# Five more seven-product pairs in a hybrid encoder layer on one Trainium2 core, with earlier sums and an unspread gate

## The chip, the core and the metric

The kernel runs on one core of a Trainium2 chip (trn2). A core has a matrix engine (TensorE, PE in the profile, with its weight loads as PEld), a vector engine (VectorE, DVE), a scalar engine (ScalarE, ACT), GpSimd (POOL) and SyncE (SP), which issues the DMAs of the weights. Each engine works through its own queue in the order of the program, and they wait for each other by semaphores. The metric is the time of one execution in device microseconds; lower is better.

## The reference

One layer of an encoder over 256 tokens of width 4096, all in float32. `h` is the normalised input; one wide projection `h @ w_in` gives latents for q and kv (1024 and 512), a rotary key (64), and gates, q, k, v for two groups of 16 heads of width 128. Group A is latent attention, group B a banded (dilated) attention over q, k, v taken straight from the projection.

```python
h = rms_norm(x, g_mix)
c_q, c_kv, k_rope, gate_a, q_b, k_b, v_b, gate_b = split(h @ w_in)
y_a = mla_attention(q from c_q @ w_uq, k and v from c_kv @ w_ukv)
y_a = rms_norm(y_a, g_out_mla) * silu(gate_a)
y_b = dilated_mixture_attention(q_b, k_b, v_b)
y_b = rms_norm(y_b, g_out_dil) * silu(gate_b)
x = x + concat(y_a, y_b) @ w_out
gate = sigmoid(rms_norm(x, g_ple) @ w_ple_gate)
x = x + (p @ w_ple) * gate
out = rms_norm(x, g_final)
```

## The kernel before, in words

**Operands in two halves.** TensorE multiplies in the reduced type fp32r. To keep float32's accuracy, every operand is split in two: `hi`, the value rounded to fp32r by ACT (L115), and `lo`, the rest, by a subtraction on DVE (L116). A product of two tiles is then three matmuls (`mm`, L133 to L135: hi times hi, hi times lo, lo times hi, of 512 columns). For weights this costs ACT and DVE one pass each over every tile that the DMA brings (`raw`).

**Blocks of 1024 columns.** A `Block` computes 256 tokens by 1024 columns of output over 32 tiles of 128 weight rows, as four quarters of 128 by 512. There are two ways to take weight rows:

- A *plain step* (`plain_step`) takes one tile of rows: four products, so eight for two tiles, and one pass of ACT and DVE over 1024 columns.
- A *fast pair* (`fast_steps`) takes two tiles of rows in four steps and needs seven products instead of eight (the scheme of Strassen and Winograd). It needs sums and differences of the four pieces of the weights, which DVE makes (four subtractions of 512 columns, L833, into a temporary tile), and of the four pieces of the left operand, which a task makes beforehand (`add_sums`, L871, with a split on ACT and DVE). So a pair has four conversions: 512 columns in the first step, 1024 in each of the others. The second step's hi half is written at L846 and its lo half at L848.

`weave(fast, lead, trail)` writes out the order of a block: `lead` plain steps, then the fast pairs with the other plain steps spread among them (the plain step stands behind the first of a pair's four), then `trail` plain steps. At the end of a block there are the tasks `mid` (when the fast products are complete) and `done`.

**The order of the program** is one list, `steps`, run from top to bottom (the loop at the end). The parts, in time: the latents and the gates of group A; 64 steps of `w_uq` and `w_ukv` beside the first half of the gate columns, in which the 16 latent heads run; the last gate columns (`ga3`, 16 steps); six blocks for q, k, v of group B (two for each, `d_mid` and `d_done`); 64 steps of group B's gate beside its heads; three blocks of `w_out` and 32 steps for its last columns; four wide blocks of `w_ple_gate` with `w_ple` (`wide_mid`, `wide_done`, `wide_ple`; the fourth has quarters of 384 columns); and the last 256 columns. The blocks of this text: the *first q block* is the first of the six; *output blocks* one to three are those of `w_out`; *wide blocks* one to four those of `w_ple_gate`.

**Lead.** At step i the loop converts up to step i + 2, or i + 5 where the block's ring has more than three places; then it emits step i's products, then calls `advance`. The *ring* names the buffers for converted operands: three of a pool (`wp`) and, where there is room, tiles that other stages leave free (`B6`, `B4`, `Ah2`, `Al1`...). A step gets no buffer until the step that had it before has run. `phase` sets the place in the ring with which a block begins; without it the count goes on. Raw tiles come by DMA, four at a time at most.

**Tasks.** Everything beside the products is a generator. `advance` (one *tick* for each step) resumes every task once, so a task's `yield` puts the rest of it behind the next step. A head (`attend`, from L409) takes one tick each for its transpositions, splits, scores, softmax, normalisation, transpositions, splits, products with v, and copy; it is flagged at its end (`("head", dil, h)`). Two heads start two ticks apart. `x_sums` makes the eight sums of x for the six q, k, v blocks, two ticks each, in tiles that the latent heads use (`T0` to `T7`, with `B0` as temporary); it waits for the last latent head, and its eighth sum for `("gated", 3)`. `y_stats` (L557) computes the root mean square of an attention's output through `rsqrt_mean` (L225, which yields three times), and `gating` (from L571) then works through four groups of heads: a scaling on ACT (L578), transpositions on PE (L585), products on DVE (L593). `wide_done` (L1063) computes a wide block's gate from four quarters: a tanh on ACT (L1084), a product on DVE (L1086), an addition to the residual (L1088), a square on ACT (L1091). From its third round on it waits five ticks in a round, except in the last block.

Of the kernel before, what the change touches and what calls it, by code (L numbers as in the profile page):

```python
# [20 lines left out]
NT = S // P  # L21
DM = 4096
HEADS = 16
# [55 lines left out]
def encoder_layer(ctx: ExitStack, tc: tile.TileContext, x, p, positions, g_mix, w_in, g_q_latent, w_uq,  # L79
# [329 lines left out]
    def attend(h, q_src, k_src, pe, v, y, dil):  # L409

        tp = turn_bank([4, P])
        for t in range(NT):
            nc.tensor.transpose(tp[:, t], q_src(t), ident)
            nc.tensor.transpose(tp[:, NT + t], k_src(t), ident)
        yield
        qk = slot(f"T{h % 2}", [2, 4 * P], F32R)
        split(qk[:, 0], qk[:, 1], tp.rearrange("p a b -> p (a b)"))  # L420
        if dil:
            flags.add(("read", h))
        yield
        s = bank("s", [NT, S])
        for t in range(NT):
            a = tuple(qk[:, i, t * P:(t + 1) * P] for i in range(2))
            b = tuple(qk[:, i, S:] for i in range(2))
            mm(s[:, t], a, b, True, pe is None)
            if pe is not None:
                both = pe[0]()[:, t * P:(t + 1) * P]  # L430
                nc.tensor.matmul(s[:, t], both, pe[1][0], start=False, stop=False)
                nc.tensor.matmul(s[:, t], both, pe[1][1], start=False, stop=True)
        yield
        i = h % 2
        e = E["t"][:, i]
        nmax, l, rl = E["s"][:, i, 0], E["s"][:, i, 1], E["s"][:, i, 2]
        if not dil:
            nc.vector.tensor_reduce(nmax, s, axis=AX.X, op=ALU.max, negate=True)
            for t in range(NT):
                nc.scalar.activation(e[:, t], s[:, t], AF.Exp, bias=nmax[:, t:t + 1], accum_out=l[:, t:t + 1])  # L440
        else:
            flat = "p a b -> p (a b)"
            nc.vector.scalar_tensor_tensor(e.rearrange(flat), E["d"][:, 0].rearrange(flat), -SLOPES[h],
                                           s.rearrange(flat), op0=ALU.mult, op1=ALU.add)
            nc.vector.tensor_reduce(nmax, e, axis=AX.X, op=ALU.max, negate=True)
            yield
            for t in range(NT):
                nc.scalar.activation(e[:, t], e[:, t], AF.Exp, bias=nmax[:, t:t + 1])
            yield
            for t in range(NT):  # L450
                nc.vector.scalar_tensor_tensor(e[:, t], e[:, t], 1.0, E["d"][:, 1, t], op0=ALU.mult,
                                               op1=ALU.mult, accum_out=l[:, t:t + 1])
            nc.vector.reciprocal(rl, l)
        yield
        if not dil:
            nc.vector.reciprocal(rl, l)
        for t in range(NT):
            if dil:
                nc.scalar.activation(e[:, t], e[:, t], AF.Copy, scale=rl[:, t:t + 1])
            else:  # L460
                nc.vector.tensor_scalar(e[:, t], e[:, t], rl[:, t:t + 1], None, op0=ALU.mult)
        yield
        tp = turn_bank([NT, S])
        for k in range(NT):
            for t in range(NT):
                nc.tensor.transpose(tp[:, k, t * P:(t + 1) * P], e[:, t, k * P:(k + 1) * P], ident)
        yield
        pt = slot(f"T{2 + h % 2}", [2, NT, S], F32R)
        split(pt[:, 0], pt[:, 1], tp)
        if dil:  # L470
            vs = slot(("Q0", "T6")[h % 2], [2, NT, HD], F32R)
            split(vs[:, 0], vs[:, 1], v)
            v = lambda kt: (vs[:, 0, kt], vs[:, 1, kt])
        yield
        o = bank("o", [S])
        for k in range(NT):
            mm(o, v(k), tuple(pt[:, i, k] for i in range(2)), k == 0, k == NT - 1)
        yield
        nc.scalar.activation(y, by_token(o) if dil else o, AF.Copy)
        sq = junk[:, S * i:S * (i + 1)] if h else acc  # L480
        nc.scalar.activation(sq, o, AF.Square)
        if h:
            nc.gpsimd.tensor_tensor(acc, acc, sq, op=ALU.add)
        flags.add(("head", dil, h))
# [72 lines left out]
    def y_stats(dil):  # L557
        while not all(("head", dil, h) in flags for h in range(HEADS)):
            yield
        yield  # L560
        tp = turn_bank([2 * S])
        for t in range(NT):
            nc.tensor.matmul(tp[:, t:t + 1], acc[:, t * P:(t + 1) * P], ones, start=True, stop=True)
        yield
        yield from rsqrt_mean(ry[dil], tp[:, :NT], WIDTH)
        nc.vector.tensor_tensor(ry[dil], ry[dil], rxh, op=ALU.mult)
        flags.add(("ry", dil))

# [494 lines left out]
    def wide_done(k, blk):  # L1063
# [10 lines left out]
        def task():  # L1074
# [7 lines left out]
            for n in range(6):  # L1082
                for i, t, h, m in quarters[n:n + 1]:
                    nc.scalar.activation(e[:, i], e[:, i], AF.Tanh, scale=r1h[:, t:t + 1])  # L1084
                for i, t, h, m in quarters[n - 1:n] if n else ():
                    nc.vector.scalar_tensor_tensor(e[:, i], e[:, i], 1.0, P4[t, h][:, :blk.q], op0=ALU.add, op1=ALU.mult)  # L1086
                    for u, xc, at, _ in pieces(h, i):
                        nc.vector.tensor_tensor(xc[:, t, at], u, xc[:, t, at], op=ALU.add)  # L1088
                for i, t, h, m in quarters[n - 2:n - 1] if n > 1 else ():
                    for u, xc, at, c in pieces(h, i):  # L1090
                        nc.scalar.activation(u, xc[:, t, at], AF.Square, accum_out=ss2[:, t, c:c + 1])  # L1091
                for _ in range(5 if n > 1 and k < WIDE - 1 else 1):
                    yield
            if k == WIDE - 1:
                for t in range(NT):
# [162 lines left out]
    lay(blk, order, gates_mid(blk), gates_done(blk))  # L1258
    hook(len(steps), only("t0", "t1"))
    M = M[::-1]  # L1260
    ga2 = from_x(OFF_GA + 1024, 512, done_gate(0, 2))
    other, ga2.banks = M
    for i in range(8):
# [2 lines left out]
        add(ga2, 2 * i + 1, 2 * i + 2)  # L1266
        add(Chunk(cols(w_ukv, 512 * i, 512), 4, 512, lhs_c("kv"), other, done_uk(i), lambda j: ["latents"]))
    hook(len(steps), lambda: spawn(y_stats(0)))
    hook(len(steps) + 1, lambda: spawn(x_sums()))
    ga3 = from_x(OFF_GA + 1536, 512, done_gate(0, 3))  # L1270
    ga3.banks = M[1]
    add(ga3)
# [2 lines left out]
    z_tags = "T0", "T1", "T2", "T3", "T4", "T7", "T5", "T6"  # L1275

    def x_sums():
        while ("head", False, HEADS - 1) not in flags:
            yield
        z = lambda j: slot(z_tags[j], [2, 4, P], F32R)  # L1280
        yield from add_sums(7, x_pair, z, "B0", "x_sums", x_s)
        while ("gated", 3) not in flags:
            yield
        yield from add_sums(8, x_pair, z, "B0", "x_sums", x_s, first=7)

    tags = LAST
    for n, key in enumerate((key, i) for i in range(2) for key in "qkv"):
        off = {"q": OFF_Q, "k": OFF_K, "v": OFF_V}[key[0]] + 1024 * key[1]
        order = weave((range(5), range(8), range(8), range(8), (4, 5, 0, 1, 2, 3, 6, 7), (0, 1, 2, 3, 6, 7))[n],
                      16 if n == 0 else 2, 2)  # L1290
        ring = (["B6", "B4"], ["B4", "B6", "B0"], ["B4", "B6", "B0"], ["B4", "B6"], ["B4", ("T4", "T7")], [("T4", "T7")])[n]
        after = ((), (), ["B4", "B6"], ["B4"], [("T4", "T7")], ())[n]
        blk = Block(w_in[:, off:off + 1024], lhs_x, x_s, "x_sums", order, lambda kt: (), tags, "B1", WP + ring)
        lay(blk, order, d_mid(key, blk), d_done(key, blk), after=after, used={2: ("used", 5)} if n == 4 else {})
        if n == 0:
            steps[-len(order[1])].phase = 0
        tags = follow(tags)
    beside = [len(steps), len(steps) + 64]
    for c in range(4):
# [7 lines left out]
    for k in range(WIDE_O):  # L1307
        hook(len(steps), only(*(("t0", "t1"), ("m2", "m3"), ("m0", "m1"))[k]))
        for h in range(2):
            hook(len(steps) + 4 + h, lambda c=2 * k + h: load_res(c))  # L1310
        order = weave(*((range(4), 12, 4), (range(7), 6, 4), (range(6), 8, 4))[k])
        blk = Block(w_out[:, 1024 * k:1024 * (k + 1)], lhs_y, y_s, "y_sums", order, lambda kt: need_y(kt // 2),
                    tags, "Al2" if k < 2 else "Al1", WP + (["Ah2", "Al1"] if k < 2 else [("B7b", "T7")]))
        lay(blk, order, out_mid(k, blk), out_done(k, blk))
        tags = follow(tags)
    for c in (6, 7):
        hook(len(steps), lambda c=c: (load_res(c), only("t0", "t1")()))
# [4 lines left out]
    for k in range(WIDE):  # L1322
# [4 lines left out]
        if k == 3:  # L1327
            hook(len(steps), lambda: spawn(load_g()))
        lay(blk, order, wide_mid(k, blk), wide_done(k, blk), wide_ple(k, q), **({"after": [], "used": {4: "z used"}} if k == 3 else {}))
    small = Chunk(cols(w_ple, 3840, 256), 2, 256, lambda kt: (pT[0][:, 0, kt], pT[0][:, 1, kt]), ("t0", "t1"), done_p(8),  # L1330
                  lambda j: ["pT"])
    steps.insert(len(steps) - 2, (small, 0))
# [235 lines left out]
```

## Time and profile before

| | us |
|---|---|
| median of 3 runs | 1924.57 (1923.02 to 1925.47) |
| the profiled execution | 1922.93 |
| its span, first to last instruction | 1921.2 |

The profile is of one execution. An engine's busy time is the sum of its instructions, and a matmul's end is modelled, so busy times of matmuls overlap and the count over a stretch tells more than the busy share. In a timeline row stand the start and the duration in us, the engine, the line of the kernel, the operation, what it writes and reads (by the program's names, numbers left out), the shape, and how many such instructions follow each other; in square brackets idle time of the engine ahead of it and what ended it. In a row of a stretch stand the stretch, its length, then busy time and count of PE, PEld, DVE, ACT and POOL, the granted clock of PE, the DMA's share and its GB/s.

### The profile page before, as it was taken

Reading aid. Unit: us, or ns where it says so; the run is one execution under the profiler, and the core shown is the slowest. Engines: PE = TensorE matmul, PEld = TensorE weight load, DVE = VectorE, ACT = ScalarE, POOL = GpSimd, SP = SyncE. Lnnn points to the kernel's source line nnn. Section 1 sums busy time; section 2 is a strip of 40 time slices with the busy share of each in tenths; the row PEclk is TensorE's granted clock in tenths of the full one; section 3 lists DMA queues with packets and bytes.
Section 4 is the critical chain, followed back from the end, with each engine's and each line's share of the span. In section 5 each row is a group of like instructions: output and inputs, shape, how many; then the busy total and the mean of one; then the engine's idle time right before and its main releaser. Section 6 shows DMA issues by size and latency. Waiting matters only on the chain.

```text
span 1921.2 us, 25661 instructions
## 1 busy us (share of the span) xinstructions
PE 1905.4 (99%) x9246; PEld 1629.2 (85%) x9246; DVE 1589.1 (83%) x2221; ACT 1114.5 (58%) x1547; POOL 71.3 (4%) x115
## 2 busy tenths in 40 slices
PE   9999999999999999999999999999999999999997
PEld 8998889998888888888888888888888888888897
DVE  7877966665999999899877778889896698989897
ACT  6655555565555565655556666555565455566554
POOL 0001011220000000000000010000000000000000
PEclk9999999999999999999999999999999999999999
DMA  7666654445656666666664456665666556566565
GB/s 260 196 181 198 206 164 145 143 153 157 196 186 206 212 209 197 214 200 196 213 195 143 132 165 219 204 213 172 233 195 217 188 190 218 183 212 202 190 220 195
DMA packets 139350, 370.58 MB, mean 193 GB/s; under 512 B 12476, under 2 KB 33816, under 8 KB 139224
## 3 DMA queue, kind: packets, MB, share of 16 engines
q1 hardware_dynamic: 137816, 363.96, 59.5%
q0 software_dynamic: 1408, 5.00, 0.7%
q8 instruction: 72, 1.18, 0.2%
q14 instruction: 54, 0.44, 0.1%
HBM read 364.72 MB, written 4.19 MB: 192 GB/s over the span
## 4 chain that ended last, share of the span: by engine, by line
PE 93%; DVE 5%; ACT 1%; issue 1%; DMA 1%; DVEq 0%; ACTq 0%
PE m L134 19%; PE m L135 19%; PE m L133 19%; PE t L133 4%; PE t L134 4%; PE t L135 4%; PE s L134 3%; PE s L135 3%; PE s L133 3%; PE o L134 3%; PE o L135 3%; PE o L133 3%; DVE lo L116 1%; DVE B L833 1%; ACT hi L115 1%
## 5 line engine op out<-in xcount | busy, mean ns | idle before, releaser
L116 DVE TENSOR_TENSOR lo<-raw,hi 128x1024 fp32r<-128x1024 f32 (+5 forms) x478 | 519.3, 1092 | 191.4 <-ACT hi L115 188.5
L115 ACT ACTIVATE hi<-raw 128x1024 fp32r<-128x1024 f32 (+5 forms) x478 | 454.0, 954 | 336.7 <-PE m L135 152.1
L133 PE MATMUL m<-hi,Ah 128*128 128x512 f32 (+3 forms) x1001 | 383.5, 383 | 0.0
L134 PE MATMUL m<-lo,Ah 128*128 128x512 f32 (+3 forms) x1001 | 378.3, 378 | 0.4 <-DVE lo L116 0.2
L135 PE MATMUL m<-hi,Al 128*128 128x512 f32 (+3 forms) x999 | 376.4, 377 | 0.0
L134 PEld LDWEIGHTS m<-lo,Ah 128*128 128x128 f32 x1001 | 188.5, 188 | 31.0 <-DVE lo L116 3.8
L135 PEld LDWEIGHTS m<-hi,Al 128*128 128x128 f32 x999 | 187.7, 188 | 31.3 <-DVE Al L127 0.7
L133 PEld LDWEIGHTS m<-hi,Ah 128*128 128x128 f32 x1001 | 188.4, 188 | 27.9 <-ACT hi L115 0.3
L133 PE MATMUL m<-hi,B 128*128 128x512 f32 (+2 forms) x429 | 163.6, 381 | 0.0
L134 PE MATMUL m<-lo,B 128*128 128x512 f32 (+2 forms) x429 | 159.9, 373 | 0.1
L135 PE MATMUL m<-hi,B 128*128 128x512 f32 (+2 forms) x429 | 159.9, 373 | 0.0
L115 ACT ACTIVATE hi<-B 128x1024 fp32r<-128x1024 f32 (+1 forms) x85 | 87.8, 1035 | 93.4 <-DVE B L833 55.2
L116 DVE TENSOR_TENSOR lo<-B,hi 128x1024 fp32r<-128x1024 f32 (+1 forms) x85 | 101.0, 1190 | 6.7 <-ACT hi L115 3.7
L833 DVE TENSOR_TENSOR B<-raw,B 128x512 f32<-128x512 f32 (+1 forms) x138 | 92.7, 671 | 0.0
L135 PEld LDWEIGHTS m<-hi,B 128*128 128x128 f32 x429 | 80.5, 188 | 11.8
L134 PEld LDWEIGHTS m<-lo,B 128*128 128x128 f32 x429 | 80.7, 188 | 11.1 <-DVE lo L116 0.6
L133 PEld LDWEIGHTS m<-hi,B 128*128 128x128 f32 x429 | 80.6, 188 | 10.5
L115 ACT ACTIVATE B<-raw 128x1024 fp32r<-128x1024 f32 (+2 forms) x68 | 61.4, 910 | 43.4 <-DMA raw<-in_w_in_dram 18.7
L115 ACT ACTIVATE B<-B 128x1024 fp32r<-128x1024 f32 (+2 forms) x62 | 59.2, 955 | 44.6 <-DVE B L833 23.8
L116 DVE TENSOR_TENSOR B<-raw,B 128x1024 fp32r<-128x1024 f32 (+2 forms) x68 | 70.2, 1038 | 11.0 <-ACT B L115 10.9
L848 DVE TENSOR_TENSOR lo<-raw,hi 128x1024 fp32r<-128x1024 f32 (+2 forms) x64 | 76.2, 1190 | 2.9 <-ACT hi L846 2.9
L116 DVE TENSOR_TENSOR T<-t,T 128x512 fp32r<-128x512 f32 x64 | 43.9, 687 | 41.6 <-ACT T L115 41.2
(769 smaller groups left out, 4020.3 us busy)
## 6 DMA issues: line engine op xcount, KB each, us to landing
raw<-in_w_in_dram SPq DMA_DIRECT2D x320, 512.0 KB, 4.0
raw<-in_w_out_dram SPq DMA_DIRECT2D x128, 512.0 KB, 4.5
raw<-in_w_ple_gate_dram SPq DMA_DIRECT2D x96, 512.0 KB, 4.6
raw<-in_w_in_dram SPq DMA_DIRECT2D x63, 400.0 KB, 3.7
raw<-in_w_uq_dram SPq DMA_DIRECT2D x32, 384.0 KB, 3.3
raw<-in_w_ple_gate_dram SPq DMA_DIRECT2D x32, 384.0 KB, 3.7
raw<-in_w_ukv_dram SPq DMA_DIRECT2D x16, 512.0 KB, 3.5
raw_l<-in_w_ple_gate_dram SPq DMA_DIRECT2D x8, 512.0 KB, 4.6
```

What stands on the lines that cost most here:

```text
L115: nc.scalar.activation(hi, src, AF.Copy)
L116: nc.vector.tensor_tensor(lo, src, plain(hi), op=ALU.subtract)
L133: nc.tensor.matmul(ps, ah, bh, start=start, stop=False)
L134: nc.tensor.matmul(ps, ah, bl, start=False, stop=False)
L135: nc.tensor.matmul(ps, al, bh, start=False, stop=stop)
L833: nc.vector.tensor_tensor(dst, a, b, op=ALU.subtract)
L848: nc.vector.tensor_tensor(lo, r[1], plain(hi), op=ALU.subtract)
```

## The change

Fast pairs: the first q block has seven in place of five and 10 plain steps ahead of them in place of 16; the first output block six in place of four (8 plain steps ahead in place of 12), the third seven in place of six (6 ahead in place of 8, 4 behind as before). `x_sums` is spawned in the last ticks of the latent stage and starts one tick after head 13 is done and head 14's scores are out. `y_stats(0)` runs its reciprocal square root in one tick. The third wide block's gate waits one tick in a round. Phases are set for 13 blocks; which buffers a block has doesn't change.

```diff
@@ attend
+        flags.add(("scored", dil, h))
         yield
@@ y_stats
-        yield from rsqrt_mean(ry[dil], tp[:, :NT], WIDTH)
+        for _ in rsqrt_mean(ry[dil], tp[:, :NT], WIDTH):
+            if dil:
+                yield
@@ wide_done
-                for _ in range(5 if n > 1 and k < WIDE - 1 else 1):
+                for _ in range(5 if n > 1 and k < WIDE - 2 else 1):
                     yield
@@ the order of the program
     M = M[::-1]
+    hook(len(steps) + 60, lambda: spawn(x_sums()))
...
     hook(len(steps), lambda: spawn(y_stats(0)))
-    hook(len(steps) + 1, lambda: spawn(x_sums()))
@@ x_sums
-        while ("head", False, HEADS - 1) not in flags:
-            yield
+        while ("scored", False, HEADS - 2) not in flags or ("head", False, HEADS - 3) not in flags:
+            yield
+        yield
@@ the six q, k, v blocks
-        order = weave((range(5), range(8), range(8), range(8), (4, 5, 0, 1, 2, 3, 6, 7), (0, 1, 2, 3, 6, 7))[n],
-                      16 if n == 0 else 2, 2)
+        order = weave((range(7), range(8), range(8), range(8), (4, 5, 0, 1, 2, 3, 6, 7), (0, 1, 2, 3, 6, 7))[n],
+                      10 if n == 0 else 2, 2)
...
-        if n == 0:
-            steps[-len(order[1])].phase = 0
+        steps[-len(order[1])].phase = (0, 0, 0, 1, 0, 2)[n]
@@ the output blocks
-        order = weave(*((range(4), 12, 4), (range(7), 6, 4), (range(6), 8, 4))[k])
+        order = weave(*((range(6), 8, 4), (range(7), 6, 4), (range(7), 6, 4))[k])
...
+        steps[-len(order[1])].phase = k
@@ the wide blocks
+        steps[-len(order[1])].phase = 3 if k else 1
```

## The prediction

> **What bounds the kernel now.** First the page: which engine is full, and which chain ends last.
>
> ```profile
> PE 1905.4 (99%) x9246; PEld 1629.2 (85%) x9246; DVE 1589.1 (83%) x2221; ACT 1114.5 (58%) x1547; POOL 71.3 (4%) x115
> ...
> PE 93%; DVE 5%; ACT 1%; issue 1%; DMA 1%; DVEq 0%; ACTq 0%
> ...
> L133 PE MATMUL m<-hi,Ah 128*128 128x512 f32 (+3 forms) x1001 | 383.5, 383 | 0.0
> ```
>
> TensorE (PE) is the bound, and the chain leaves it for VectorE (DVE) in 5% only. The 383 ns of a matmul are no price, though: matmuls overlap. The pace is read from stretches, as time over count.
>
> ```profile
> 660.00:741.00 81.00, 81.00 (x359) 67.11 (x358) 75.47 (x88) 46.71 (x49) 0.00 (x0) 1.00 0.65 202
> ...
> 447.00:480.00 33.00, 33.00 (x168) 27.97 (x167) 17.81 (x24) 15.42 (x28) 3.52 (x3) 1.00 0.51 155
> 494.60:522.00 27.40, 27.40 (x132) 22.61 (x131) 25.27 (x48) 16.19 (x20) 0.00 (x0) 1.00 0.65 195
> ...
> 1303.00:1368.00 65.00, 65.00 (x289) 53.83 (x287) 60.76 (x71) 37.32 (x40) 1.44 (x2) 1.00 0.60 201
> ```
>
> The columns are the stretch, its length, then busy time and count of PE, PEld, DVE, ACT and POOL. The first stretch is a block of eight fast pairs: 81.0 / 359 = 0.226 us a matmul at full clock (1.00), with DVE 93% busy, and PE never waits. So fast pairs can be hidden; what decides is whether DVE, which prepares their operands, keeps ahead. Next, the two engines where the chain leaves PE, in the first q block (487 to 579 us). PE first:
>
> ```profile
> 531.75 0.39 PE L135 MATMUL o<-hi,Al 128*128 128x512 f32 x1
> ...
> 532.34 0.49 PE L133 MATMUL m<-B,Ah 128*128 128x512 f32 x1
> ...
> 535.20 0.39 PE L133 MATMUL m<-B,Ah 128*128 128x512 f32 x1
> ...
> 548.12 0.39 PE L133 MATMUL m<-B,Ah 128*128 128x512 f32 x1
> 548.42 0.50 PE L134 MATMUL m<-B,Ah 128*128 128x512 f32 x1
> ...
> 563.67 0.39 PE L133 MATMUL m<-B,Ah 128*128 128x512 f32 x1
> 564.11 0.50 PE L134 MATMUL m<-B,Ah 128*128 128x512 f32 x1
> ```
>
> The first number is the start. A group of transpositions between 531.75 and 532.34 costs 0.59 - 0.23 = 0.4 us. At 535.20 the first fast step starts. At 548.12 a lo half comes late (0.30 instead of 0.23), and at 563.67 too (0.44): the first and the last of three such places. With the next matmul, which each time comes 0.1 late as well, they cost about 0.3 us in each fast group from the third on, 0.85 in all. DVE beside it:
>
> ```profile
> 478.76 0.68 DVE L871 TENSOR_TENSOR B<-Ah,Al 128x512 f32<-128x512 f32 x1
> ...
> 531.38 0.86 DVE L593 SCALAR_TENSOR_TENSOR B<-B,gT,t 128x256 f32<-128x256 f32 x2
> ...
> 535.25 0.68 DVE L833 TENSOR_TENSOR B<-raw 128x512 f32<-128x512 f32 x1
> ...
> 537.05 0.68 DVE L871 TENSOR_TENSOR B<-Ah,Al 128x512 f32<-128x512 f32 x1
> 537.77 1.02 DVE L871 TENSOR_TENSOR B<-B 128x128 f32<-128x128 f32 x4
> ...
> 539.85 0.68 DVE L116 TENSOR_TENSOR T<-B,T 128x512 fp32r<-128x512 f32 x1
> ...
> 545.34 0.69 DVE L833 TENSOR_TENSOR B<-raw 128x512 f32<-128x512 f32 x1
> ...
> 553.18 0.69 DVE L833 TENSOR_TENSOR B<-raw 128x512 f32<-128x512 f32 x1
> ...
> 554.40 1.82 DVE L116 TENSOR_TENSOR B<-raw,B 128x512 fp32r<-128x512 f32 x2
> 556.14 0.68 DVE L833 TENSOR_TENSOR B<-raw,B 128x512 f32<-128x512 f32 x1
> 556.74 1.21 DVE L848 TENSOR_TENSOR lo<-raw,hi 128x1024 fp32r<-128x1024 f32 x1
> 557.87 0.68 DVE L833 TENSOR_TENSOR B<-raw,B 128x512 f32<-128x512 f32 x1
> 558.48 2.52 DVE L116 TENSOR_TENSOR lo<-B,hi 128x1024 fp32r<-128x1024 f32 x2
> 561.02 0.69 DVE L833 TENSOR_TENSOR B<-raw 128x512 f32<-128x512 f32 x1
> ```
>
> From 553.18 to 561.02 DVE never rests: a fast pair and the plain step among its four cost it 7.84 us, of which the plain one is 1.2, so 6.6 a pair. PE needs 33 x 0.226 = 7.45. Where pairs follow each other with one plain step each, DVE loses about 0.3 to 0.4 us a group, and PE pays as soon as DVE's lead is used up.
>
> **The change part by part.**
>
> *Five products less.* Two pairs in the first q block, two in the first output block, one in the third: 5 x 3 = 15 matmuls of 512 columns, 15 x 0.226 = **-3.4 us**. The Trainium skill (Trainium Kernel Development and Optimization, Performance Expectations) says that matmul busy time is a bad metric because matmuls are pipelined; by the 383 ns the sum would be -5.7, by the pace it is -3.4, and this trace agrees with the rule (359 x 0.383 us is far more than 81). The Trainium skill (TensorE: Matmul & The Clock Gate, Wait — 56ns, not 53.3ns?) gives 215.7 ns for such a start to start; by it the term would be -3.2, and here the measured pace decides.
>
> *First q block: new stalls.* Each pair added takes 6.6 - 2 x 1.2 = 4.2 us more of DVE, 8.4 in all. The first fast step comes six plain steps sooner, 6 x 12 x 0.226 = 16.3 us, and two groups of transpositions now lie behind it (0.8): 535.2 - 17.1 = 518.1. The sums of x (2.3 us each: 0.68, 1.02 and 0.68, slightly overlapped) start at 478.76 now, when the last head is done. After, they start one tick behind the third last head, and heads are two ticks apart: three ticks sooner. A tick is one step of PE here, 2.7 us and some transpositions, so 9 us: in a stretch where DVE is busy 17.8 of 33 us, which hides them. Six more sums of two ticks each, and the seventh is ready by about 506, ahead of the dense stretch. The gating, too, starts three ticks sooner (the three yields of the rsqrt). The first fast step moves by 17 us and the gating by 9, so against it the gating is 8 us later: its last two pairs of L593 (0.8 each) fall into the dense stretch, where they were ahead of it, beside the eighth sum, which was in it already. The second group's conversion can't start sooner than the first fast step itself, since it takes the buffer of the step five before (535.25 beside 535.20); so the third group's comes 1.6 us later than now, against 0.8 that PE spends on the transpositions. Third group: 0.2 + 0.8 = 1.0; four more at 0.3: 2.2 in place of 0.85, so **+1.4 us** (0.7 if the gating is out of the way, 2.4 if the transpositions don't help).
>
> *First output block.* There the DVE was full before; where is it now?
>
> ```profile
> 1201.69 0.48 PE L133 MATMUL m<-hi,B 128*128 128x512 f32 x1
> ...
> 1238.18 0.39 PE L133 MATMUL m<-Al,B 128*128 128x512 f32 x1
> ...
> 1217.65 1.23 DVE L116 TENSOR_TENSOR Al<-raw,Al 128x1024 fp32r<-128x1024 f32 x1
> ...
> 1227.62 0.69 DVE L871 TENSOR_TENSOR T<-B 128x512 f32<-128x512 f32 x1
> ```
>
> The block starts at 1201.69 and reaches its first fast step at 1238.18, behind 13 plain ones; after, behind 8, at 1224.6. DVE converts the ninth step at 1217.65, so the first pair is converted from there: 7.8 us with its plain step, 2 x 0.8 of gating, 2 x 0.6 of splits, and the seventh sum (2.3, at 1227.62 now). That ends at 1230.6, and the second group's first two steps at 1233.6; PE wants that at 1224.6 + 7.45 + 0.9 = 1233.0 to 1233.5. About **+0.3 us**; the third group has two plain steps and gives back 1.5. Bounds 0 and 1.5 (DVE one sum later).
>
> *Third output block.* Seven pairs with 6 and 4 plain steps outside is just the weave of the second block, whose stretch (1303 to 1368) has 65 / 289 = 0.225 us a matmul, no stall. It has one buffer fewer in its ring, so two steps less of slack to lose 0.3 a group from: **+0.1 us** (0 to 0.5).
>
> *Gate of the third wide block unspread.* In the last block DVE is full and PE waits for it:
>
> ```profile
> 1832.35 0.33 PE L133 MATMUL m<-B,Ah 128*128 128x384 f32 x1
> 1832.72 0.44 PE L134 MATMUL m<-B,Ah 128*128 128x384 f32 x1
> ...
> 1837.86 0.34 PE L133 MATMUL m<-B,Ah 128*128 128x384 f32 x1
> 1838.95 0.45 PE L134 MATMUL m<-B,Ah 128*128 128x384 f32 x1 [0.75 <-DVE B L116]
> ...
> 1828.97 0.69 DVE L1086 SCALAR_TENSOR_TENSOR B<-B,junk 128x512 f32<-128x512 f32 x1
> ...
> 1830.31 0.55 DVE L833 TENSOR_TENSOR B<-raw 128x384 f32<-128x384 f32 x1
> ...
> 1836.61 0.68 DVE L1086 SCALAR_TENSOR_TENSOR B<-B,T 128x512 f32<-128x512 f32 x1
> 1837.94 0.95 DVE L116 TENSOR_TENSOR B<-raw,B 128x768 fp32r<-128x768 f32 x1
> ```
>
> Two pieces of the gate, 1.34 us each, lie right ahead of the conversions for which PE stands 0.2 us at 1832.35 and 0.9 us at 1837.86 (0.1 more each on the next matmul). Unspread, both come by 1826, where PE is still in the plain steps; what they delay there has over 1 us to spare. Both stalls go: -1.3, and of the smaller ones behind them some 0.3: **-1.6 us** (-2.2 to -0.5, if the conversions stay late for their raw tiles).
>
> *The rest at nothing.* The phases set where a ring of buffers begins; no row shows one, and a buffer that comes round a step early costs at most a stall like those above: 0, bounds -0.5 and +0.5. The flag and the hook issue no instruction.
>
> Sum: -3.4 + 1.4 + 0.3 + 0.1 - 1.6 = **-3.2 us**; the bounds of the terms give -5.4 to +1.0. The profiled execution took 1922.93 us (span 1921.2), so 1919.7; the median shown is 1924.57, 1.6 above it, and so I forecast 1921.4 as a median, with 1919.2 to 1925.6 by the bounds.
>
> **The rivals.**
> *All is hidden* (0.20). The eight-pair block shows 93% DVE without a stall; if the gating stays ahead of the fast stretch, nothing new appears: -3.4 - 1.6 = -5.0, 1919.6. Against it: the 7.84 us period with one plain step a group.
> *The lead is lost* (0.11), the slower side. At the first fast step DVE must be five steps ahead: a pair's 6.6 us and three passes of 0.6 of the next, 8.5 us. Between 494.6 and 522 it is busy 25.3 of 27.4 us now, and the fast conversions move into this. Were the moved sums held up (each waits in DVE's one queue for a tile that the last two heads still read, with the conversions behind it), up to 16 us of sums would stand ahead of the first conversions, and the whole lead could be gone: -3.2 + 8.5 = +5.3, 1929.9. It decides for slower once 7 us of the lead are missing. Against it: heads and sums keep to the same ticks, and DVE is half idle before 480.
> *Stalls twice as large* (0.05) in the three blocks: -1.4, 1923.2.
> *The pairs don't run as such in time* (0.02): a sum that is flagged late is made right ahead of its product, 2.3 us each; for one, -0.9, 1923.7. Against: by the ticks above each sum is out before its group is converted.
>
> **How the numbers follow.** A measurement of this kernel can tell 0.2%, 3.85 us, from no change. My forecast has 0.62, 1919.2 to 1925.6; of it 0.22 lies beyond -3.85 and 0.40 within. Faster: 0.22 + 0.20 = 0.42. Same: 0.40 + 0.05 + 0.02 = 0.47. Slower: 0.11. The range 1918.5 to 1926.0 holds the forecast, the hidden case and the two small ones.
>
> **What would show it.** Right: 15 matmuls less; in the first q block three to five late lo halves at 0.2 to 0.5 us, none before the third group; no late lo half at the two places of the last block; L593's last pairs behind the second fast conversion. Wrong: a matmul gap over 1 us in the q or output blocks, a DVE wait for PE in the moved sums, or the last block's stalls still there.

## The result, and the profile after

The changed kernel takes **1934.92 us** (median of 5 runs, 1934.24 to 1935.13), the kernel before 1923.62 beside it (5 runs, 1922.59 to 1925.47): a ratio of **1.0057, interval 1.0042 to 1.0072**. It is 11.3 us slower; 3.2 us less were forecast, in a range that ended at 1926.0.

The page of the changed kernel, the same rows as before:

```profile
span 1933.0 us, 25677 instructions
...
PE 1907.1 (99%) x9231; PEld 1628.9 (84%) x9231; DVE 1611.9 (83%) x2251; ACT 1122.3 (58%) x1557; POOL 73.3 (4%) x115
...
PE 90%; DVE 6%; DMA 2%; ACT 1%; issue 1%; DVEq 0%; POOL 0%; ACTq 0%; SPq 0%
```

The 15 matmuls are gone (9246 to 9231), and the span is 11.8 us longer (1921.2 to 1933.0). PE still looks 99% busy, since the share is rounded: its busy time rose by 1.7 us, although there are 15 matmuls less, and its idle time (span less busy time) rose from 15.8 to 25.9 us. What is new stands in the chain: DMA went from 1% to 2%, PE from 93% to 90%. To find the place, take the start-to-start distances of PE's instructions, subtract the pace of their shape, and sum by stretch. Two stretches show it: 475 to 575 us (1.4 before, 7.9 after) and 1425 to 1475 (0.2 before, 8.5 after). The stretches of the changed kernel around these two places, in the columns of the prediction's first rows:

```profile
514.00:521.40 7.40, 7.40 (x40) 6.13 (x39) 5.51 (x10) 4.50 (x6) 0.00 (x0) 1.00 0.25 76
521.40:527.70 6.30, 1.35 (x6) 0.52 (x4) 6.30 (x11) 2.44 (x3) 0.00 (x0) 0.80 0.53 162
527.70:531.70 4.00, 4.00 (x10) 3.13 (x11) 2.58 (x6) 1.02 (x2) 0.00 (x0) 0.50 0.43 138
531.70:540.00 8.30, 8.30 (x37) 6.87 (x36) 7.71 (x10) 4.68 (x7) 0.00 (x0) 0.98 0.37 101
1450.00:1456.30 6.30, 6.30 (x29) 5.22 (x28) 0.72 (x1) 3.02 (x3) 1.45 (x2) 1.00 0.84 255
1456.30:1461.70 5.40, 0.40 (x2) 0.00 (x0) 3.81 (x6) 1.06 (x1) 0.00 (x0) 0.88 0.23 91
1461.70:1467.00 5.30, 5.26 (x12) 4.14 (x13) 5.30 (x7) 0.16 (x1) 0.00 (x0) 0.50 0.63 198
```

Both places have the same form: full pace; then 5 to 6 us in which PE issues almost nothing; then 4 to 5 us at a granted clock of **0.50**, in which 10 matmuls take 4.0 us and 12 take 5.3, instead of 0.226 each; then full pace again. The second half of the loss is the clock: (4.0 - 10 x 0.226) + (5.3 - 12 x 0.226) = 1.7 + 2.6 us. The Trainium skill (TensorE: Matmul & The Clock Gate, HAM oscillation — how this bites in real kernels) says that PE must have no idle gaps over some 3.4 us, or its clock is halved. This trace agrees with it at the second place, where the gap is 5.2 us. At the first it doesn't fit so simply: the clock is down to 0.50 from 525.1 on, 1.2 us after the last matmul began (523.98), so the gap of 3.5 us can't have done it alone, and the one of 1.8 us just ahead of it must count as well. The last section comes back to this.

**The first place: a PSUM bank shared by two stages.** PE in the first fast group of the first q block (idle time ahead, and what ended it, in brackets), with DVE below (the lines of the changed kernel have numbers three higher: L836 is L833 of before, L596 is L593):

```profile
518.01 0.39 PE L133 MATMUL m<-hi,Ah 128*128 128x512 f32 x1
...
521.43 0.40 PE L135 MATMUL m<-hi,T 128*128 128x512 f32 x1
523.44 0.47 PE L133 MATMUL t<-hi,T 128*128 128x512 f32 x1 [1.62 <-DVE B L596]
523.75 0.40 PE L134 MATMUL t<-lo,T 128*128 128x512 f32 x1
523.98 0.39 PE L135 MATMUL t<-hi,T 128*128 128x512 f32 x1
527.70 0.76 PE L133 MATMUL t<-hi,T 128*128 128x512 f32 x1 [3.33 <-DVE B L596]
...
521.83 0.68 DVE L116 TENSOR_TENSOR lo<-raw,hi 128x512 fp32r<-128x512 f32 x1
522.43 0.86 DVE L596 SCALAR_TENSOR_TENSOR B<-B,gT,t 128x256 f32<-128x256 f32 x2
523.21 1.22 DVE L116 TENSOR_TENSOR B<-raw,B 128x1024 fp32r<-128x1024 f32 x1
524.35 0.68 DVE L836 TENSOR_TENSOR B<-raw,B 128x512 f32<-128x512 f32 x1
524.95 1.22 DVE L851 TENSOR_TENSOR B<-raw,B 128x1024 fp32r<-128x1024 f32 x1
526.08 0.68 DVE L836 TENSOR_TENSOR B<-raw,B 128x512 f32<-128x512 f32 x1
526.68 0.87 DVE L596 SCALAR_TENSOR_TENSOR B<-B,gT,t 128x256 f32<-128x256 f32 x2
```

The fast steps begin at 518.01, where the prediction put them (518.1), and the gating's pairs (L593 before, L596 now) come among the fast conversions, as it said. What it did not say is who waits for them. PE's waiting matmuls write `t`: the banks `t0` and `t1`, which hold two of the seven products of this block (`LAST` ends with them), and are also where the gating puts its transpositions. A product can't begin in such a bank until L596 has read the transposition out of it. L596 stands in DVE's one queue, behind conversions of the second group: 1.8 us for the first bank, 3.5 for the second. Before, the gating's last read ended at 535.3, ahead of the first product in such a bank (537.92).

**The second place: a tile that holds a sum and a residual.** The chain of the changed kernel in the third output block (start, length, engine, what):

```profile
1450.13 0.24 PE m L135
1450.37 0.29 issue
1450.66 0.72 POOL T L727
1451.38 7.74 DMA T<-in_x_dram
1459.12 0.02 issue
1459.14 0.70 DVE T L941
...
1460.47 1.23 DVE lo L116
1461.70 0.04 issue
1461.74 0.80 PE m L134
```

The rows of POOL beside it, first after and then before:

```profile
1450.66 1.45 POOL L727 DMA_DIRECT2D T<-in_x_dram  x2 [285.30 <-PE m L135]
```

```profile
1360.31 1.44 POOL L724 DMA_DIRECT2D T<-in_x_dram  x2 [200.18 <-PE o L135]
```

The residual of x for output columns 2048 to 2559 goes into tile T4 (`load_res`); the seventh sum of y is in T4 as well (the end of `y_sums`). With six pairs the third block didn't use that sum, and T4 was free before this block began: the load left at 1360, 85 us ahead of its first use (1445.23). With a seventh pair T4 is free only when that pair has run, near the block's end: the two loads leave at 1450.66 and 1451.38 and land 6.9 and 7.7 us later, L941 (the block's addition to the residual) waits for them in DVE's queue, and the conversions of the following steps stand behind L941. PE waits 5.2 us and then has half its clock.

**The rest.** In the first output block a conversion comes late, 0.36 and 0.93 us (1238.45 to 1239.61 below), 1.5 in all with 0.1 on each next matmul. In the last block the two stalls of before are gone: the second of its two quoted matmuls came 1.09 us behind the first before, and comes 0.17 behind it now (1851.50).

```profile
1238.45 0.40 PE L133 MATMUL m<-hi,B 128*128 128x512 f32 x1
1239.61 0.50 PE L134 MATMUL m<-lo,B 128*128 128x512 f32 x1 [0.76 <-DVE lo L116]
...
1851.50 0.33 PE L133 MATMUL m<-B,Ah 128*128 128x384 f32 x1
1851.67 0.33 PE L134 MATMUL m<-B,Ah 128*128 128x384 f32 x1
```

Sum, in us of the span: -3.4 (matmuls) + 6.5 (first q block) + 1.5 (first output block) + 8.4 (third) - 1.6 (last block) = +11.4, of 11.8.

### The profile page after: what moved, and what is told of

Read it like the earlier page. It is cut to its first block, busy times and chain, and to the rows that moved or that the text cites. A ratio compares the mean times of both kernels' runs of the same rounds, so it can differ in the third digit from the quotient of the medians.

```text
span 1933.0 us, 25677 instructions
## 1 busy us (share of the span) xinstructions
PE 1907.1 (99%) x9231; PEld 1628.9 (84%) x9231; DVE 1611.9 (83%) x2251; ACT 1122.3 (58%) x1557; POOL 73.3 (4%) x115
## 4 chain that ended last, share of the span: by engine, by line
PE 90%; DVE 6%; DMA 2%; ACT 1%; issue 1%; DVEq 0%; POOL 0%; ACTq 0%; SPq 0%
PE m L134 19%; PE m L135 18%; PE m L133 18%; PE t L133 4%; PE t L135 4%; PE t L134 4%; PE s L134 3%; PE s L133 3%; PE s L135 3%; PE o L134 3%; PE o L135 3%; PE o L133 3%; DVE lo L116 2%; DVE B L836 1%; ACT hi L115 1%
## 5 line engine op out<-in xcount | busy, mean ns | idle before, releaser
L115 ACT ACTIVATE hi<-B 128x1024 fp32r<-128x1024 f32 (+1 forms) x89 | 92.3, 1039 | 99.1 <-DVE B L836 53.5
L116 DVE TENSOR_TENSOR lo<-B,hi 128x1024 fp32r<-128x1024 f32 (+1 forms) x89 | 106.1, 1193 | 8.0 <-ACT hi L115 4.8
L836 DVE TENSOR_TENSOR B<-raw,B 128x512 f32<-128x512 f32 (+1 forms) x142 | 95.8, 674 | 0.0
L116 DVE TENSOR_TENSOR B<-raw,B 128x1024 fp32r<-128x1024 f32 (+2 forms) x62 | 66.0, 1066 | 11.5 <-ACT B L115 11.3
```

Of the source, the lines that this page charges most:

```text
L115: nc.scalar.activation(hi, src, AF.Copy)
L116: nc.vector.tensor_tensor(lo, src, plain(hi), op=ALU.subtract)
L836: nc.vector.tensor_tensor(dst, a, b, op=ALU.subtract)
```

## The experiments

Theory: the two long gaps, each from a resource shared by two stages (bank, tile), cost about 15 us, and without them the forecast holds. Rival: DVE's lead is lost in these blocks, and gaps only move when one cause is taken away.

**Third output block: the sum in T4 used first.** On the changed kernel:

```diff
-(range(7), 6, 4))[k]
+((6, 0, 1, 2, 3, 4, 5), 6, 4))[k]
```

> The changed kernel with one edit: in the third output block the seventh pair runs first instead of last, so the tile of its sum (T4) is free for the residual's load early in the block. The weave, the count of pairs and DVE's work stay. Buffer theory (the residual's DMA waits for T4, DVE's queue waits for the DMA, PE for DVE): the gap of 5.2 us near 1456 us goes, and with it the half clock behind it (some 2.0 us) and the late half of 0.4: 1934.9 - 7.5 = 1927.4 us. Lead theory (seven pairs are too dense for a ring of four): the block is as dense as before, so no change, 1934.9.

Measured: 1931.53 us (4 runs, 1930.36 to 1932.27; before 1923.54), ratio 1.0039 (1.0024 to 1.0054). The gap of 5.2 us and the half clock behind it are gone, so T4 was the cause. But only 3.4 us came back, of 8.4: by the profiles 5.5 are back in this block, while 3.5 were lost anew in the last one. The load now leaves early in the block, beside the weights; the DMAs issued from 1395 to 1412 us in this kernel, and before:

```profile
raw<-in_w_out_dram SPq DMA_DIRECT2D x5, 512.0 KB, 7.4
T<-in_x_dram POOLq DMA_DIRECT2D x2, 512.0 KB, 8.4
```

```profile
raw<-in_w_out_dram SPq DMA_DIRECT2D x6, 512.0 KB, 4.2
```

The weights land after 7.4 us in place of 4.2, and PE waits for their halves (0.6 + 1.0 us at 1410). A late landing alone isn't enough for that: before, beside the same two loads at 1360, a weight tile took 7.9 us, and PE didn't wait. The profile also has a new gap of 1.6 + 0.8 us in the last block, at 1873, and behind it the granted clock is 0.50 for 3.4 us, without any gap near 3.4 us:

```profile
1872.50:1875.80 3.30, 1.29 (x6) 0.85 (x6) 1.08 (x2) 1.84 (x3) 0.00 (x0) 1.00 0.96 363
1875.80:1879.20 3.40, 3.40 (x12) 3.40 (x11) 3.33 (x6) 1.76 (x3) 0.00 (x0) 0.50 0.86 268
```

**First q block: the gating one tick sooner** (changed kernel, in `y_stats`, ahead of the scaling):

```diff
-            yield
+            if dil:
+                yield
```

> The changed kernel with one edit: group A's gating drops the tick ahead of its scaling, four ticks over its four groups, so its last two products on DVE come ahead of the first q block's fast pairs. Bank theory (the first products of M7 and M6 go to the PSUM banks t1 and t0, where the gating's transposed tiles still wait for DVE): both gaps near 521 and 524 us (1.8 and 3.5) and the half clock behind them (2.0) go, late lo halves of 1 to 2 us come from the third group on: 1934.9 - 7.3 + 1.0 = 1928.6 us. Lead theory (DVE is late with the fast conversions): only 1.6 us of DVE work leaves the dense stretch, 1933.3.

Measured: 1931.49 (4 runs, 1929.18 to 1933.08), ratio 1.0039 (1.0024 to 1.0054). Both waits for L596 and the half clock are gone: the bank theory holds. What is left in this block are late lo halves of 0.2 us; two of the five, 532.34 and 555.88, in PE's rows:

```profile
531.95 0.39 PE L133 MATMUL m<-hi,Ah 128*128 128x512 f32 x1
532.34 0.50 PE L134 MATMUL m<-lo,Ah 128*128 128x512 f32 x1
...
555.42 0.39 PE L133 MATMUL m<-hi,Ah 128*128 128x512 f32 x1
555.88 0.50 PE L134 MATMUL m<-lo,Ah 128*128 128x512 f32 x1
```

They come every 7.8 us, three groups apart here, which is DVE's 7.84 us a group. The time is 2.9 above what was expected; the profiled execution, the fastest of the four, is only 0.6 above (1929.18), so what the others lost stands in no profile.

**The unspread gate alone** (the kernel before with only that line of the diff):

> The kernel before with one edit: the third wide block's gate unspread. Theory that two of its pieces stand ahead of late conversions: -1.6 us against before (1922.0 where before is 1923.6), with the two late lo halves of the last block gone. Rival that the conversions stay late for their raw tiles: -0.5 or nothing.

Measured: 1922.02 (10 runs, 1921.33 to 1923.10; before 1923.54), ratio 0.9990 (0.9981 to 1.0000). The -1.6 of the forecast is -1.5, with an interval that just reaches no change; both named stalls are gone from its profile.

**Of the pairs only the first output block's** (changed kernel, first q block back to `range(5)`, 16 ahead; third output block back to `(range(6), 8, 4)`):

> The changed kernel with the first q block back at five pairs behind 16 plain steps and the third output block back at six: what is left are two pairs in the first output block, the earlier sums, the short rsqrt, the phases and the unspread gate. Buffer and bank theory: no long gap anywhere; two pairs -1.4, DVE late in the first output block +1.4, gate -1.7: 1923.6 - 1.7 = 1921.9 us. Rival that the moved sums or the phases cost time by themselves: over 1923.6.

Measured: 1923.28 (10 runs, 1921.22 to 1925.01), ratio 0.9997 (0.9987 to 1.0007). No long gap in the q and output blocks: the two changes that were undone hold both. But it is 1.4 above the expectation, and its profile again has a gap in the last block (1.6 + 0.8 us). From 450 to 600 us its stalls are 0.8, against 1.6 before: the earlier sums and the short rsqrt cost nothing there.

**Both repairs, and three variants of the output blocks.** First, the changed kernel with the two edits above. Second, this with 10 plain steps ahead in the first output block (in place of 8). Third, the second with the loads of the third block's two residuals in the other order. Fourth, the sooner gating, the 10 plain steps, and the third block back to six pairs:

```diff
-weave(*((range(6), 8, 4), (range(7), 6, 4), (range(7), 6, 4))[k])
+weave(*((range(6), 10, 4), (range(7), 6, 4), (range(6), 8, 4))[k])
```

> The changed kernel with both edits: seventh pair first in the third output block, and the gating one tick a group sooner. Both long gaps should be gone together. Against before, from the gaps seen in the single edits: 15 matmuls -3.4, late lo halves of the first q block +0.7, of the first output block +1.5, the third output block's late raw tiles +2.6, gate unspread -1.5: -0.1, so 1923.4 us. If the two long gaps had a common cause that only moves from one place to the other, a gap of over 3 us stays and the time is 1927 or more.

> As the kernel with both edits, and the first output block's six pairs behind 10 plain steps instead of 8 (two fewer among them). Theory that the wait of 0.45 and 0.93 us at its second group comes of group B's last splits and the seventh sum, which DVE still has to do when the first pair is converted: two plain steps later (5.5 us) they are over, and of 1.5 us about 0.3 are left: 1922.2 us. Rival that the denser weave is what DVE can't follow: the stall moves behind the second group and is as large or larger, 1923.4 or more.

> As the kernel with 10 plain steps, and of the third output block's two residual loads the one that needn't wait for T4 is issued first. Theory that in the kernel with the seventh pair first the raw tiles come late (7.4 us instead of 4.2) because both residual loads run beside them in the dense stretch: one of them now comes early, in the plain steps, and of the block's 2.6 us about half goes: 1.3 us less than with 10 plain steps alone, 1920.9 us. Rival that those raw tiles are late for another reason: no change.

> Gating one tick a group sooner, first output block behind 10 plain steps, and the third output block back at six pairs behind 8 (four pairs added instead of five, T4 free as before). 12 matmuls -2.7, late lo halves +0.7 and +0.3, gate unspread -1.5: -3.2 against before, 1920.3 us. If the seventh pair in the third block is worth its product in spite of its loads, this is slower than the kernel whose free load goes first.

Measured, 11 runs each, before 1923.91: 1925.82, ratio 1.0010 (1.0001 to 1.0018); 1926.31, 1.0012 (1.0003 to 1.0021); 1925.83, 1.0008 (0.9999 to 1.0017); 1924.36, 1.0000 (0.9991 to 1.0009). All four miss by 2.4 to 4.9 us: with the two long gaps gone, about nine or more of the eleven lost microseconds are back, but no gain is left. My theory was thus incomplete. In the first three the residual's load in the third block still costs 2.1 to 2.7 us in the stretch from 1400. The order of the two loads made no difference: in the third kernel one of them left at 1157 already, the one into T4 went alone at 1398, and that stretch lost 2.5 us, against 2.1 with both; so it doesn't take two loads side by side, as that theory had it. With 10 plain steps ahead the wait of 0.9 us at the first output block's second group is gone, as expected, but late halves of 0.2 us stay (1.1 us of stalls in the block in place of 1.5), and the time is no better. In the third kernel a weight also lands late in that block (6.8 us, with waits of 0.5 and 1.0 us at 1269), for which no run shows the reason. The last kernel has no such cost in the third block and is 1.5 to 2.0 us faster than the other three by the medians, so the seventh pair there isn't worth its product; yet it gains nothing over before. Its chain in the last block:

```profile
1857.93 0.48 DVE lo L116
1858.41 0.02 issue
1858.43 8.42 DMA raw<-in_w_ple_gate_dram
1866.85 0.02 issue
...
1866.95 0.85 ACT hi L115
```

A weight tile takes 8.4 us to land, and PE waits for its halves (0.95 and 0.82 us at 1865 and 1866). It lands beside the eight loads of `g_final` (2 MB, `load_g`), which SP issues in the same stretch. Its own issue also took SP 1.49 us.

**The g_final loads two ticks apart.** A base (before, unspread gate, this edit), the base with the first q block's pairs and the sooner gating, and the last kernel above with this edit; beside them, that last kernel with the gate spread again and no such edit:

```diff
@@ load_g, behind each load
-            yield
+            yield from [None] * 2
```

> The kernel before, with the unspread gate and the eight loads of g_final (beside the last wide block) two steps of the order apart in place of one, so that they no longer stand ahead of the last raw loads of w_ple_gate in SP's queue. Broadcast theory (the 2 MB of g_final, landing beside the last raw loads, hold these back): the unspread gate alone had no gap of that kind in its profile, so 1922.0 +-0.5, as without the edit. Rival (the gap in the last block has nothing to do with these loads): the same 1922.0 here; this one is the base of the next two.

> The same g_final loads and unspread gate, with the first q block's two further pairs, the earlier sums of x and the sooner gate of the gating; output blocks as before. Six matmuls fewer are -1.4; the late lo halves at 525 to 565 cost +1.4 in the profiles of the repaired kernels. Theory that these sizes add up: 1922.0 +-0.5, no gain over the base. Rival (the q pairs gain what was forecast of them without the bank's wait, -1.4 and nothing lost): 1920.6.

> The repaired kernel (sooner gating, first output block's two further pairs from step 10, third output block as before) with the g_final loads two steps apart. Broadcast theory: the gap of 0.95 + 0.82 us at 1865 in the last block goes, and 1924.4 becomes 1922.3 or so. Rival (the raw load is late because it is issued later in the order): the gap stays and the time with it, 1924.4.

> The repaired kernel with the gate of the third wide block spread as before, g_final loads as before. If the gap in the last block comes from the unspread gate (its raw loads move against the g_final loads): the gap of 1.8 goes, the spread gate costs its 1.5, 1924.1 or a little less. If the gap has nothing to do with the gate: it stays and 1.5 come on top, 1925.9.

Measured, 11 runs each, before 1923.88:

| kernel | us | ratio |
|---|---|---|
| base | 1921.58 | 0.9991 (0.9982 to 0.9999) |
| base, first q block's pairs | 1921.97 | 0.9990 (0.9981 to 0.9999) |
| repaired, g_final apart | 1922.02 | 0.9990 (0.9981 to 0.9999) |
| repaired, gate spread | 1925.08 | 1.0006 (0.9997 to 1.0015) |

The third line is the answer: 1924.36 becomes 1922.02. The landing times of `raw` from 1850 to 1872 us, in the repaired kernel without the edit and then with it:

```profile
DMA to landing us min/median/max: 2.6/4.2/8.4
```

```profile
DMA to landing us min/median/max: 3.8/4.4/5.4
```

The slowest tile lands after 5.4 us in place of 8.4, and the gap is gone. With the gate spread it stays (1.56 + 0.82 us in its profile), so the gate isn't its cause; the time lies between the two that were expected, and it is the profile that decides. The base keeps a small one (0.8 us at 1862). Nor do the pairs of a particular block account for it: the profile of the kernel before and that of the changed one don't have it, although SP's order of the loads is the same. The traces do show where it differs. In all six profiles with the large gap (with no spacing of the loads) SP took 0.8 to 1.6 us to issue the late weight load itself, and it landed after 7.7 to 8.5 us; in the five without the gap only loads of `g_final` took SP so long (1.0 to 1.3 us), every weight load was issued in 0.33 to 0.38 us, and the slowest landed after 6.0 to 7.0 us. Why the long issue falls on the one or the other stays open. Each kernel has one profile only, and executions of one kernel lie up to 5.0 us apart (1922.58 to 1927.61 with the gate spread again) where the loads are not spaced, 1.5 to 2.7 where they are; so the gap may well come and go between executions, which no profile here shows.

And the base is as fast as either kernel with more pairs. In the third one, the stretches of fast steps in the first q block and the first output block:

```profile
519.00:578.00 59.00, 58.76 (x254) 46.97 (x253) 58.28 (x73) 33.79 (x38) 0.00 (x0) 1.00 0.60 186
1240.00:1290.00 50.00, 49.88 (x219) 40.33 (x218) 49.44 (x59) 29.42 (x34) 0.00 (x0) 1.00 0.65 211
```

DVE is busy 58.28 of 59.00 us and 49.44 of 50.00. In the first, 59.0 - 254 x 0.2256 = 1.7 us of PE's time are stalls; by all starts from 450 to 600 us they are 3.0, against 1.6 before. Six matmuls less are worth 6 x 0.226 = 1.4 us, and DVE takes 1.4 back. In the base DVE is busy 54.71 and 44.59 us of the same two stretches. In the first output block the two pairs bring 1.4 and cost 1.0.

## Why the prediction was wrong

Two steps of the sum failed, in the first q block and in the third output block. Both counted what the engines have to do and left out what two stages share, a bank and a tile.

- **Five products less, -3.4**: right, 15 matmuls at 0.226.
- **First q block, +1.4**: its mechanism was right and had the right size, in the kernels without the bank's wait: +1.4 by all starts. The exact agreement is luck: the block's five late lo halves cost about 0.33 us each, 1.6 against 2.2 in the forecast, with none of 1.0 in the third group, and the rest comes from one more at the start of the next block (579) and small stalls ahead of 515. The step that failed is another: "against it the gating is 8 us later: its last two pairs of L593 (0.8 each) fall into the dense stretch". It priced these pairs as 1.6 us of DVE's work. They also hold the banks in which two products begin, and so each became a wait of PE's: 1.8 + 3.5 us, and 1.7 of half clock. I moved a task past a block without asking which banks the two share.
- **First output block, +0.3**: a conversion is late, as it said, but it costs 1.5 us, the upper bound given. The mechanism held; the size was that of the bound. That one sum was the reason is not shown; two plain steps later the wait is gone.
- **Third output block, +0.1**: wrong, and the largest error (+8.4). The step was "just the weave of the second block". The weave is the same, the block isn't: its seventh pair reads a sum in a tile that the next residual needs. The working looked at conversions alone and never asked what a further pair keeps occupied, and until when.
- **Unspread gate, -1.6**: right, -1.5 alone (-1.6 in the changed kernel's last block), and both named stalls are gone.
- **The rest at nothing**: no run varied the phases alone, so that is open. Left out was the collision at the end of the kernel, up to 2.4 us and in one profile a slower clock behind it, which is in some of these profiles and not in others; a forecast to a few microseconds should have had it in its range.
- **The rivals.** "All is hidden" fails on the 7.84 us period, as the prediction argued. "The lead is lost" had the right sign and 1929.9, but not the mechanism: DVE doesn't wait in the moved sums; PE waits for a bank, and DVE for a load that waits for a tile. No rival had a shared resource in it, and none had the price of a long wait, which includes the clock. "A matmul gap over 1 us in the q or output blocks" was named as what would show the forecast wrong, and that is what the trace shows.

With its two overlooked waits out, the forecast's terms give -3.2 + 0.7 - 0.1 = -2.6 us for the repaired kernel with six pairs in the third block (one pair less, and its stall), and with the `g_final` loads apart it takes -1.9 (1922.02 against 1923.88). That these are close doesn't confirm the terms of the pairs: the base, with the gate and the spaced loads and no pair more, takes -2.3 by itself (1921.58). The four pairs were priced at -2.7 + 1.4 + 0.3 = -1.0 in it; over the base they measure +0.4, which is not clear of no change. By the stalls of the profile they are worth -2.7 + 1.4 + 1.0 = -0.3.

## What to carry to other kernels

When a stage is lengthened or moved, list what it holds (banks, tiles, buffers) and who needs each next: a further step in a block can be free on every engine and still keep a tile for 90 us longer. Price a long wait of the matrix engine with the slower clock that can follow it, here 1.4 to 2.6 us more. And where the vector engine is already full, taking matmuls away at its expense gained nothing here: look at its busy share in the very stretch first.

## What the runs showed of the hardware

- The clock beside long waits. In the changed kernel the granted clock is 0.50 from 525.13 to 531.96 and from 1460.38 to 1467.21 us, 6.83 us each time, of which PE works the last 4 to 5. The same two waits were followed by only 3.41 us of it in other profiles: the first from 527.54 to 530.95 with the seventh pair first, the second from 1456.39 to 1459.81 with the gating sooner. They cost about 1.4 us there, in place of 1.7 and 2.6.
- In each profile all changes of the clock lie whole multiples of 3.413 us apart (6.83, 928.43 and 6.83 in the changed kernel: 2, 272 and 2 of them). In the 3.41 us ahead of a fall PE had done little: 3 matmuls from 521.71 to 525.13, none from 1456.97 to 1460.38, and 5 of 384 columns from 1872.39 to 1875.80 in the kernel with the seventh pair first (at full pace 0.20, 0 and 0.25 of that time). Where it had worked for 0.42 of it (520.71 to 524.12, same kernel) or 0.46 (1866.79 to 1870.20, the kernel with the gate spread again), the clock stayed at 1.00, although the latter has the same gaps of 1.6 and 0.8 us. So what counted in these profiles is PE's work in such a step of 3.41 us, and whether a gap falls into one step or across two, rather than the length of a gap. This is a reading of the traces; no run varied it.
- Loads beside a stream of weights. With two loads of 512 KB issued from POOL beside them, weight tiles of 512 KB landed after 7.4 and 7.8 us, where the median before was 4.2 in that stretch; with one such load the late tile took 7.4. Eight loads of 256 KB on SP's own queue went with a landing of 8.4 us in the last block, in place of 5.4 at most when they were two ticks apart, without one byte less.
- SP's issues: the late weight load took SP 1.49 us to issue where the others took 0.33, so part of the delay is in the issue itself. In all six profiles with the gap that issue took 0.8 us or more.
